# Low parts of half-size weight blocks: a negated copy and an accumulating transfer in place of subtractions on GpSimd

## The chip, the cores and the metric

The kernel runs on one core of one Trainium2 chip. The metric is the device time of one execution in microseconds; the time before is 1047.58 us, the median of three runs (1045.82 to 1047.79).

A core has five engines that run their own instruction queues in order: TensorE (PE, with its weight loads as PEld), VectorE (DVE), ScalarE (ACT), GpSimd (POOL) and SyncE (SP). They wait for each other by semaphores. Transfers run on 16 DMA engines; they are issued by an instruction on the queue of SP or ACT and, after the change, also on that of POOL.

## The reference

One inference step of two layers over 1024 prompt tokens and 8 x 4 sample tokens (1056 columns in all), d_model 1024, in float32. The first layer is a gated linear recurrence (RG-LRU), the second, which the change concerns, an HGRN2 layer:

```python
def _hgrn_layer(x, g_norm, w_in, lb, o_gain, w_out, S0):
    xn = _rmsnorm(x, g_norm)
    u = (xn @ w_in).astype(jnp.float32)          # w_in: 1024 x 4096
    q, f, iv, gate = jnp.split(u, 4, axis=-1)
    q = jax.nn.silu(q).reshape(Bsz, T, H_B, DK_B)            # 8 heads of 128
    ...                                                      # log_g from f and lb; k = -expm1(log_g)
    o, S_T = _hgrn2_chunked(q, k, v, log_g, S0)
    o = o * lax.rsqrt(jnp.mean(o * o, axis=-1, keepdims=True) + EPS) * o_gain...
    y = (o.reshape(Bsz, T, INNER_B) * jax.nn.silu(gate)).astype(x.dtype)
    return x + y @ w_out, S_T.astype(x.dtype)
```

## The kernel before

**Three matmuls for a product.** Float32 products are made from operands of type float32r. Each operand is split into a high part (the value, rounded by a copy to float32r) and a low part (value minus high part). `mm3` (L255 to L257) then adds high x high, high x low and low x high into one PSUM bank. So every block of weights needs a high part `hi` (tile `whi`) and a low part `lo` (tile `wlo`) before PE can use it.

**Weights.** A block comes from HBM into a raw buffer (`wraw`; in the second layer two further raw buffers lie in rows of the tile `R`). ACT copies it to `hi`; POOL (or DVE, at a few places) subtracts `hi` from it into `lo` (`subtract`, L339). `hi` and `lo` have rings of NW = 4 blocks of 512 columns each, used in turn by all blocks. `weights` (with its copy on L394) does this for ordinary products. It is the first layer's way and also that of the output projection at the end.

**Seven products for eight.** From the third head on all four parts of the second layer's input projection, and two of the second head's, are computed by `seven`, 13 calls in all. A call takes two blocks of 128 output rows by 1024 inputs, thus four half-size blocks "11", "12", "21", "22" of 128 x 512. Four combinations of them (`combine`, L1458, on DVE, in the raw buffers themselves; the fifth raw buffer is "s") let seven products stand for eight. The products are numbered 1 to 7; 1 and 2 use "11" and "12" as loaded, 6, 7, 5 and 3 use combined blocks, 4 uses "22". The order is a string such as `126b754b3`, where a `b` is a burst of the attention part of a head. Each product is done twice, over 264 columns (`x` 0 and 1), so a half is 4 x 3 matmuls. `plus` (L1521, DVE) and a copy on ACT (L1493, product 1) empty the PSUM banks, of which three are used in turn for these products.

**The split.** `split(p)` makes the high and low part for product p: a copy on ACT (L1448) and the subtractions on POOL, in CUT = 2 pieces of 256 columns. There are 13 x 7 = 91 splits. The next splits of a call are entered four products ahead, as the ring allows:

```python
for p in steps[2:NW]:
    split(p)
...
n = steps.index(p) + NW
if n < 7:
    split(steps[n])
```

A raw buffer that has had its last split is handed on (`freed`, `rawq`); the next call's loads, issued on ACT's queue, go into it once the split's reads are done. `combine` likewise overwrites a raw buffer only after the splits that read it.

**The order of work.** Nothing is issued in the order in which the code is written. `fl.add(engine, us, emit, reads, writes, priority, kb)` enters each step with an estimated duration (`act`, `dve`, `pool`, `dma`) and what it reads and writes; `Flow.run` plans the start of all steps by these estimates, improves the plan by passes from the end and by a random search, and then emits each engine's instructions in the planned order. One plan covers the first layer, a second one the rest. PE's products keep their order; the other engines' instructions do not.

Of the kernel before, what the change touches and what calls it, by code (L numbers as in the profile page):

```python
# [18 lines left out]
AF = mybir.ActivationFunctionType  # L19
ALU = mybir.AluOpType  # L20
# [3 lines left out]
SEARCH = 3000  # L24
NW, NXO, NRAW = 4, 3, 3
K1 = 5
NMM = 3
HC = 2
NM7 = 3
FQ, GV0, GV = "12b675b43", "126b74b35", "126b754b3"  # L30
CUT = 2
SPOTS, SPOTS0, SPOTS1 = (-1, -1, 0, 2), (2, 5, -1, -1), (1, 5, 9, 13, 17, 20)
K2 = 8 - K1
RM, SM = 3, 6
# [189 lines left out]
def tile_trunk(ctx: ExitStack, tc: tile.TileContext, xT, prm, hc, w0, wg, wo0, w1, wo1, s_in,  # L224
               yT, h_out, c_out, sp_out, ss_out):
    nc = tc.nc
    V, S, G, T, Q = nc.vector, nc.scalar, nc.gpsimd, nc.tensor, nc.sync
# [22 lines left out]
    def chunk(c):  # L250
        return slice(c * CH, (c + 1) * CH)

    def mm3(out, w, xh, xl, first, last):
        wh, wl = w
        T.matmul(out, wh, xh, start=first, stop=False)  # L255
        T.matmul(out, wh, xl, start=False, stop=False)  # L256
        T.matmul(out, wl, xh, start=False, stop=last)  # L257
# [53 lines left out]
    with ExitStack() as l0:  # L311
        pl = l0.enter_context(tc.tile_pool(name="l0", bufs=1, reuse_waits="tile"))
        fl = Flow("PE")

        def fixed(name, shape, dt=F32, pool=None):
            return (pool or pl).tile(shape, dt, tag=name, name=name)
# [7 lines left out]
        def dma(dst, src, r=(), w=(), prio=5, kb=180, q=Q):  # L324
            fl.add("SP" if q is Q else "ACT", 0.45, lambda: q.dma_start(dst, src), r, w, prio, kb * (1.0 if r or fl.exact else 0.75))

        def act(n, emit, r, w, prio=5, more=0.0):
            fl.add("ACT", (0.09 + 0.00088 * n if fl.exact else 0.25 + 0.0007 * n) + more, emit, r, w, prio)

        def dve(n, emit, r, w, prio=5, both=False):  # L330
            own = 0.135 if "scalar_tensor_tensor" in emit.__code__.co_names else 0.085
            fl.add("DVE", own + 0.00107 * n if fl.exact else 0.13 + 0.0011 * n, emit, r, w, prio, both=both)

        def pool(n, emit, r, w, prio=5):
            fl.add("POOL", 0.13 + 0.0022 * n if fl.exact else 0.1 + 0.00245 * n, emit, r, w, prio)

        def subtract(e, n, b, x, a, r, w, prio):

            emit = lambda: e.tensor_tensor(b, x, a.bitcast(F32), op=ALU.subtract)  # L339
            if e is G:  # L340
                pool(n, emit, r, w, prio)
            else:
                dve(n, emit, r, w, prio, True)
# [38 lines left out]
        def weights(src, n, prio=2, e=G, at=None, q=Q, own=()):  # L382

            own = iter(own)
            got = []
            for a in range(0, n, 512):
                m = min(512, n - a)
                raw, *rk = next(own, None) or next(raws)
                if at:
                    (hi, hk), (lo, lk) = ((o[:, a:a + m], k) for o, k in at)  # L390
                else:
                    (hi, hk), (lo, lk) = next(his), next(los)
                dma(raw[:, :m], src[:, a:a + m], (), rk, prio, m / 2, q)
                act(m, lambda hi=hi, raw=raw, m=m: S.copy(hi[:, :m], raw[:, :m]), rk, (hk,), prio)  # L394
                subtract(e, m, lo[:, :m], raw[:, :m], hi[:, :m], (*rk, hk), (lk,), prio)
                got.append((hi, lo, hk, lk))

            def get(k):
                q = slice((k % 4) * 128, (k % 4 + 1) * 128)
                hi, lo, hk, lk = got[k // 4]  # L400
                return hi[:, q], lo[:, q], (hk, lk)

            return get
# [18 lines left out]
        def project0(items):  # L422

            for src, evac in items:
                w = weights(src, 1024)
                for c in range(NCH):
                    evac(c, *product(w, xcols(c)))
                    yield
# [432 lines left out]
        raw = (halves[1][:8], [slots[i] for i in (1, 4, 7, 2, 5, 8)] + [halves[1][8], free[8]], free[:8])  # L861
# [82 lines left out]
    with ExitStack() as l1:  # L944
        p1 = l1.enter_context(tc.tile_pool(name="l1", bufs=1, reuse_waits="tile"))
        last = {e: max(t[3] for t in fl.log if t[1] == e) for e in Flow.ENGINES}
        fl = Flow(side=0.4, busy={e: max(0.0, t - last["PE"]) for e, t in last.items()})
        banks8 = [next(mm) for _ in range(4)] + [next(hg) for _ in range(4)]
        mm, hg = cycle(banks8[:NMM]), cycle(banks8[NMM:])
        ts = cycle(ks)  # L950
# [3 lines left out]
        at = fixed("attn", [128, 8, 128], F32, p1)  # L954
# [30 lines left out]
        def pe(us, emit, r, w):  # L985
            fl.add("PE", us, emit, r, w, 1, main=True)
# [16 lines left out]
        def inherit(new, olds):  # L1003

            fl.readers.setdefault(new, []).extend(i for k in olds for i in (*fl.readers.get(k, ()), *([fl.writer[k]] if k in fl.writer else [])))
# [3 lines left out]
        def ykeys(m, a, n):  # L1009

            return [("Y", m, i) for i, (u, v) in enumerate(zip(CUTS, CUTS[1:])) if u < a + n and v > a]
# [409 lines left out]
        def seven(h, a, b, order, at=()):  # L1421
# [24 lines left out]
            def split(p):  # L1446
                (raw, rk), (hi, hk), (lo, lk) = slot[named[p]], next(his), next(los)
                act(512, lambda: S.copy(hi, raw), (rk,), (hk,), 2)  # L1448
                for i in range(CUT):
                    w = slice(i * (512 // CUT), (i + 1) * (512 // CUT))  # L1450
                    subtract(G, 512 // CUT, lo[:, w], raw[:, w], hi[:, w], (rk, hk), (lk,), 2)
                parts[p] = hi, lo, (hk, lk)
                if p not in (1, 2):
                    freed.append(slot[named[p]])
# [15 lines left out]
            for c in order:  # L1470
# [8 lines left out]
                hi, lo, wk = parts[p]  # L1479
# [36 lines left out]
                n = steps.index(p) + NW  # L1516
# [72 lines left out]
        for k in range(H):  # L1589
            if k < 4:  # L1590
                olds = [("x", 1, k, x) for x in range(2)] + [("T", 1, i, k, x) for i in range(2) for x in range(2)]
            else:
                n, i = ((2, 0), (3, 0), (4, 0), (4, 1))[k - 4]
# [18 lines left out]
        def yparts(c):  # L1612
            return [(yh[k][:, chunk(c)], yl[k][:, chunk(c)], (("yh", k, c), ("yl", k, c))) for k in range(K1)]

# [12 lines left out]

        mm, hg = cycle(banks8[:NMM]), cycle(banks8[NMM:])
        raws = cycle([r for r in rawq if r[1][0] == "raw"])
# [6 lines left out]
        for n, (m, c) in enumerate([(m, c) for c in range(NCH) for m in range(2)] + [(m, c) for m in range(2, KD) for c in range(NCH)]):  # L1636
            if m not in ws2:
                at_ = None
                if m < 2:
                    at_ = [(flat[m + 2, 1][:, i * 640:i * 640 + 640], ("wt", m, i)) for i in range(2)]  # L1640
                    for _, k in at_:
                        inherit(k, [("T", m + 2, 1, j, x) for j in range(4) for x in range(2)])
                ws2[m] = weights(wo1[m][:, :128 * K1], 128 * K1, at=at_)
                for k in ykeys(Y2 + m, 0, TOK):
# [15 lines left out]
        for m in range(KD):  # L1660
            row = (xh, xl)[m // 4][4 + m % 4]
            hi, lo, hk, lk = row[:, :nl], row[:, nl:2 * nl], ("late", m, 0), ("late", m, 1)
            for k in (hk, lk):
                inherit(k, [("x", p, m % 4, x) for p in (2, 3) for x in range(2)])
            raw, rk = next(raws)
            dma(raw[:, :nl], wo1[m][:, 128 * K1:], (), (rk,), 1, nl / 2)
            act(nl, lambda hi=hi, raw=raw: S.copy(hi, raw[:, :nl]), (rk,), (hk,), 1)
# [58 lines left out]
        for a, n in OUT:  # L1726
# [4 lines left out]
            for m in range(KD):  # L1731
# [5 lines left out]
                hi, lo, wk = late[m]  # L1737

                def emit(ps=ps, hi=hi, lo=lo, q=q, n=n):
                    for k in range(K2):  # L1740
                        w = slice(128 * k, 128 * k + 128)
                        mm3(ps[:, :n], (hi[:, w], lo[:, w]), yh[K1 + k][:, q], yl[K1 + k][:, q], k == 0, k == K2 - 1)

                pe(9 * n / 2200, emit, (*wk, *((o, K1 + k, c) for o in ("xh", "xl") for k in range(K2) for c in cs)), (pk,))
                x, xk = x2[m][:, q], ykeys(Y2 + m, a, n)
# [89 lines left out]
```

## The time and the profile before

| | |
|---|---|
| median of 3 runs | 1047.58 us (1045.82 to 1047.79) |
| span of the profiled execution, first to last instruction | 1045.1 us; its own time around the span is not recorded, the three runs lie 0.7 to 2.7 us above the span |
| busy: PE, DVE, ACT, POOL | 1033.6, 824.2, 582.9, 511.3 us |
| first and last start of the changed copy L1448 | 548.2 and 902.0 us |

A row of a group reads: line, engine, operation, output tile <- inputs, shapes, count | busy us, mean ns of one | idle time of the engine just before them, and who ended it. A row of waits reads: who waited, for whom: us in total, times, longest. A row of the timeline begins with its start and its length in us. Transfers have the size in KB and the median time from issue to landing in us. The table of stretches gives each engine's busy time with its number of instructions.

### The profile page before, as it was taken

The page shows a single profiled execution, that of the slowest core. Times are in us where ns is not written, and L with a number is a line of the kernel's source. Part 1 is how long each engine was busy: PE and PEld are TensorE (multiplying, and loading weights), DVE is VectorE, ACT ScalarE, POOL GpSimd, SP SyncE. Part 2 cuts the span into 40 slices and gives each one's busy share as a digit, 9 for nine tenths or more (in the row PEclk, how much of TensorE's full clock was granted, in tenths as well). Part 3 has the DMA queues.
Part 4 walks back from the last instruction along what each step waited for, and adds up shares of the span by engine and source line. Part 5 has one row for each costly group of instructions (what it writes and reads, how often), then busy time and mean ns, then how long its engine had stood idle before and what let it go on. Part 6 is the DMA issues. An engine that isn't in the chain of part 4 may idle for free.

```text
span 1045.1 us, 25638 instructions
## 1 busy us (share of the span) xinstructions
PE 1033.6 (99%) x9860; PEld 1004.5 (96%) x9860; DVE 824.2 (79%) x1620; ACT 582.9 (56%) x1327; POOL 511.3 (49%) x587
## 2 busy tenths in 40 slices
PE   9999999999999999999999999999999999999997
PEld 9999999999999999999999999999999999999986
DVE  7999996788788689345598998988979797985436
ACT  6568656867765776334455464546463645652324
POOL 3425343544435365644517655555555565651544
PEclk9999999999999999999999999999999999999998
DMA  9201112123761586435646142423324242576204
GB/s 303 66 20 55 54 49 72 49 65 97 214 197 48 170 281 195 145 118 173 195 138 187 56 131 97 129 85 116 97 101 127 88 127 85 182 224 210 86 1 167
DMA packets 92010, 130.67 MB, mean 125 GB/s; under 512 B 11632, under 2 KB 70000, under 8 KB 91888
## 3 DMA queue, kind: packets, MB, share of 16 engines
q1 hardware_dynamic: 82096, 112.64, 34.7%
q10 hardware_dynamic: 9792, 16.40, 5.0%
q8 instruction: 77, 1.26, 0.5%
q14 instruction: 45, 0.37, 0.1%
HBM read 85.93 MB, written 38.20 MB: 119 GB/s over the span
## 4 chain that ended last, share of the span: by engine, by line
PE 88%; DVE 8%; DMA 2%; issue 1%; POOL 0%; ACTq 0%; ACT 0%; POOLq 0%; SPq 0%; DVEq 0%
PE mm L255 25%; PE mm L257 24%; PE mm L256 24%; PE hg L1075 2%; PE hg L583 1%; PE hg L1289 1%; DMA wraw<-in_w_dram 1%; PE hg L255 1%; PE hg L1291 1%; PE hg L256 1%; PE hg L257 1%; DVE a L1257 1%; DVE sg L1057 1%; DVE R L1057 1%; PE hg L1333 1%
## 5 line engine op out<-in xcount | busy, mean ns | idle before, releaser
L255 PE MATMUL mm<-xh,whi 128*128 128x352 f32 (+1 forms) x1127 | 352.5, 313 | 0.7 <-DVE k L1521 0.5
L257 PE MATMUL mm<-xh,wlo 128*128 128x352 f32 (+1 forms) x1127 | 346.9, 308 | 0.0
L256 PE MATMUL mm<-xl,whi 128*128 128x352 f32 (+1 forms) x1127 | 346.7, 308 | 0.0
L339 POOL TENSOR_TENSOR wlo<-wraw,whi 128x256 fp32r<-128x256 f32 (+3 forms) x188 | 203.9, 1100 | 207.1 <-ACT whi L394 103.0
L255 PEld LDWEIGHTS mm<-xh,whi 128*128 128x128 f32 x1127 | 211.7, 188 | 3.2 <-DVE k L1521 1.6
L256 PEld LDWEIGHTS mm<-xl,whi 128*128 128x128 f32 x1127 | 212.0, 188 | 1.5
L257 PEld LDWEIGHTS mm<-xh,wlo 128*128 128x128 f32 x1127 | 211.8, 188 | 0.0
L255 PE MATMUL mm<-t,whi 128*128 128x264 f32 (+1 forms) x330 | 96.5, 292 | 0.8 <-DVE k L1521 0.8
L515 DVE SCALAR_TENSOR_TENSOR k<-xb,prm_sb,k 128x352 f32<-128x352 f32 (+2 forms) x144 | 89.5, 633 | 9.6 <-ACT k L512 6.4
L257 PE MATMUL mm<-t,wlo 128*128 128x264 f32 (+1 forms) x330 | 94.5, 286 | 0.0
L256 PE MATMUL mm<-t,whi 128*128 128x264 f32 (+1 forms) x330 | 94.3, 286 | 0.0
L339 POOL TENSOR_TENSOR wlo<-R,whi 128x256 fp32r<-128x256 f32 x70 | 63.7, 931 | 47.6 <-ACT whi L1448 30.7
L1521 DVE TENSOR_TENSOR k<-mm,k 128x264 f32<-128x264 f32 x154 | 64.2, 423 | 16.5 <-PE mm L257 15.8
L598 POOL TENSOR_TENSOR k<-X 128x352 f32<-128x352 f32 x36 | 42.8, 1199 | 47.7 <-DVE R L599 38.8
L255 PEld LDWEIGHTS mm<-t,whi 128*128 128x128 f32 x330 | 62.0, 188 | 1.6 <-DVE k L1521 1.0
L257 PEld LDWEIGHTS mm<-t,wlo 128*128 128x128 f32 x330 | 62.1, 188 | 0.2 <-POOL wlo L339 0.2
L256 PEld LDWEIGHTS mm<-t,whi 128*128 128x128 f32 x330 | 62.1, 188 | 0.0
L394 ACT CAST whi<-wraw 128x512 fp32r<-128x512 f32 (+2 forms) x79 | 43.8, 572 | 29.9 <-PE mm L256 15.9
L1448 ACT CAST whi<-wraw 128x512 fp32r<-128x512 f32 x56 | 34.4, 616 | 33.2 <-DVE wraw L1458 13.5
L255 PE MATMUL mm<-yh,whi 128*128 128x352 f32 x153 | 49.9, 326 | 0.0
L257 PE MATMUL mm<-yh,wlo 128*128 128x352 f32 x153 | 49.4, 323 | 0.0
L256 PE MATMUL mm<-yl,whi 128*128 128x352 f32 x153 | 49.4, 323 | 0.0
(457 smaller groups left out, 2540.3 us busy)
## 6 DMA issues: line engine op xcount, KB each, us to landing
wraw<-in_w_dram SPq DMA_DIRECT2D x53, 256.0 KB, 3.1
wraw<-in_w_dram ACTq DMA_DIRECT2D x37, 256.0 KB, 2.9
wraw<-in_wo_dram SPq DMA_DIRECT2D x34, 192.0 KB, 2.5
R<-in_w_dram ACTq DMA_DIRECT2D x17, 256.0 KB, 2.9
si<-in_s_in_dram SPq DMA_DIRECT2D x8, 512.0 KB, 6.6
vt<-sg SPq DMA_DIRECT2D x8, 512.0 KB, 3.1
sg<-vt SPq DMA_DIRECT2D x32, 128.0 KB, 3.0
kt<-kt SPq DMA_DIRECT2D x8, 512.0 KB, 2.6
```

The source lines that it names most:

```text
L255: T.matmul(out, wh, xh, start=first, stop=False)
L256: T.matmul(out, wh, xl, start=False, stop=False)
L257: T.matmul(out, wl, xh, start=False, stop=last)
L339: emit = lambda: e.tensor_tensor(b, x, a.bitcast(F32), op=ALU.subtract)
L394: act(m, lambda hi=hi, raw=raw, m=m: S.copy(hi[:, :m], raw[:, :m]), rk, (hk,), prio)
L515: dve(u, lambda src=src, dst=dst, sh=sh, k=k: V.scalar_tensor_tensor(dst, sh(src, k), pc("cw", 12 * k + m), dst, op0=ALU.mult, op1=ALU.add ...
L583: fl.add("PE", 0.62, lambda ps=ps, i=i, c=c: T.matmul(ps[:96, :CH], gs[:, i, :], ST[:96, chunk(c)], start=True, stop=True), (("gs",), *((" ...
L598: pool(CH, lambda x=x, a=a, b=b: G.tensor_tensor(x, a.bitcast(F32), b.bitcast(F32), op=ALU.add), (ak, bk), (xk,), 3)
L1057: dve(n // 2, lambda sv=sv, dv=dv, s=s, f=f: V.tensor_tensor(dv[:, :, s, :], sv[:, :, s, :], f, op=ALU.mult), (*sk, *gk), dk if i == o els ...
L1075: T.matmul(ps[32 * j:32 * j + 32, n * w:n * w + w], B[:, o:o + 32], q(slice(o, o + 32)), start=True, stop=True, tile_position=(0, 32 * j))
L1448: act(512, lambda: S.copy(hi, raw), (rk,), (hk,), 2)
L1521: dve(QT, lambda: V.tensor_tensor(o[0], z[0], u[0], op=ALU.add), (z[1], u[1]), (o[1],), 0)
```

## The change

`split` no longer subtracts on POOL. ACT writes the negated raw block into `lo` (a second pass over the 512 columns, which does not need `hi` as an input), rounded as the high part is; then a transfer issued on POOL's queue adds the raw block to it, within SBUF. `remainder` and `swdge` are new; the plan counts 1.1 us of POOL for the issue, and for the landing what it counts for other transfers. The raw buffer is now read by the transfer, so it is free when that has landed. A branch in `weights` that would do the same stays off, as `FIRST` is true.

```diff
+FIRST = True
...
+        def swdge(dst, src, r, w, prio, kb, op=None):
+            more = {"accum_op": op} if op else {}
+            fl.add("POOL", 1.1, lambda: G.dma_start(dst, src, **more), r, w, prio, kb)
+
+        def remainder(n, lo, raw, r, lk, prio):
+
+            act(n, lambda: S.activation(lo, raw, AF.Copy, scale=-1.0), r, (lk,), prio)
+            swdge(lo, raw, (*r, lk), (lk,), prio, n / 2, ALU.add)
...
-                subtract(e, m, lo[:, :m], raw[:, :m], hi[:, :m], (*rk, hk), (lk,), prio)
+                if e is G and at is None and not FIRST:
+                    remainder(m, lo[:, :m], raw[:, :m], rk, lk, prio)
+                else:
+                    subtract(e, m, lo[:, :m], raw[:, :m], hi[:, :m], (*rk, hk), (lk,), prio)
...
             def split(p):
                 (raw, rk), (hi, hk), (lo, lk) = slot[named[p]], next(his), next(los)
                 act(512, lambda: S.copy(hi, raw), (rk,), (hk,), 2)
-                for i in range(CUT):
-                    w = slice(i * (512 // CUT), (i + 1) * (512 // CUT))
-                    subtract(G, 512 // CUT, lo[:, w], raw[:, w], hi[:, w], (rk, hk), (lk,), 2)
+                remainder(512, lo, raw, (rk,), lk, 2)
                 parts[p] = hi, lo, (hk, lk)
```

## The prediction

> **What bounds the kernel now.** I read the page first, then the table of stretches, then who waited for whom on PE in the stretch that the change touches.
>
> ```profile
> span 1045.1 us, 25638 instructions
> PE 1033.6 (99%) x9860; PEld 1004.5 (96%) x9860; DVE 824.2 (79%) x1620; ACT 582.9 (56%) x1327; POOL 511.3 (49%) x587
> core 0: us, PE busy (x) PEld busy (x) DVE busy (x) ACT busy (x) POOL busy (x), PEclk, DMA share, GB/s
> 548.00:908.00 360.00, 359.30 (x5036) 346.40 (x5035) 312.16 (x644) 190.68 (x505) 206.62 (x245) 1.00 0.36 115
> 908.00:950.00 42.00, 40.09 (x570) 38.02 (x569) 35.52 (x79) 19.62 (x60) 18.73 (x21) 1.00 0.64 196
> ```
>
> TensorE has work in 99% of the span. All 91 splits that are changed start between 548 and 902 us. In the stretch 548 to 908 PE is idle for 0.70 of 360 us, at a granted clock of 1.00. DVE is next (312 us), then POOL (207) and ACT (191). So POOL, which the change relieves, doesn't set the end; relief can reach the time only through PE's waits. First the stretch's own, then those of 905 to 923 us:
>
> ```profile
> PE mm L255 <- DVE k L1521: 0.5, 2, 0.2
> PEld mm L255 <- DVE k L1521: 1.6, 4, 0.5
> PE mm L255 <- DVE k L1521: 1.9, 2, 1.1
> PEld mm L255 <- ACT whi L394: 1.3, 1, 1.3
> PEld mm L255 <- DVE k L1521: 1.0, 1, 1.0
> ```
>
> In the stretch PE waited four times for a PSUM bank that DVE had not emptied (L1521), at most 1.6 us in all as the weight loads show it. Behind it come two waits, 1.3 + 1.0 = 2.3 us. The most that any relief can give is 1.6 + 2.3 = 3.9 us.
>
> **The change part by part.** First what is removed and what stands for it, by kind and shape:
>
> ```profile
> L339 POOL TENSOR_TENSOR wlo<-wraw,whi 128x256 fp32r<-128x256 f32 x112 | 102.1, 931 | 95.7 <-ACT whi L1448 73.0 <-PE mm L257 7.0 <-DVE a L1257 4.8
> L339 POOL TENSOR_TENSOR wlo<-R,whi 128x256 fp32r<-128x256 f32 x70 | 63.7, 931 | 47.6 <-ACT whi L1448 30.7 <-PE mm L257 6.3 <-PE hg L1333 4.0
> L1317 POOL TENSOR_TENSOR rst<-rst,mhalf 128x4 f32<-128x4 f32 x12 | 12.2, 1015 | 11.5 <-DVE rst L1315 11.5
> L1448 ACT CAST whi<-wraw 128x512 fp32r<-128x512 f32 x56 | 34.4, 616 | 33.2 <-DVE wraw L1458 13.5 <-PE mm L256 12.7 <-PE mm L257 4.4
> L1448 ACT CAST whi<-R 128x512 fp32r<-128x512 f32 x35 | 21.7, 621 | 28.5 <-PE mm L256 17.2 <-POOL wlo L339 6.0 <-PE mm L257 4.4
> ```
>
> - Removed: 112 + 70 = 182 subtractions on POOL, 102.1 + 63.7 = 165.8 us, two for each of the 91 splits.
> - Added on ACT: 91 passes of the shape of the high part's copy. 34.4 + 21.7 = 56.1 us is what 91 of those take, so ACT goes from 191 to about 247 us of 360 (69%). It lies beside PE's work; ACT also empties some banks (L1493) and issues the weight loads, so its queue is a rival below.
> - Added on POOL: 91 transfer issues. No row shows GpSimd issuing a transfer. The bounds are 0.33 us (an issue on ACT's queue, quoted below) and 1.86 (the two subtractions that it replaces). I take 1.0, by L1317: 1015 ns for 4 elements per partition, so nearly all fixed cost. POOL then falls from 207 to about 207 - 166 + 91 = 132 us.
> - Added to the DMA engines: 91 x 256 KB = 23.9 MB, 66 GB/s over 360 us beside the 115 in the table. By bytes the DMA share goes from 0.36 to 0.57, or to 0.78 if reading the destination counts as much again. This leaves room, but single loads will land later than now.
>
> The landing time of an accumulating transfer is shown by no row either. The nearest:
>
> ```profile
> wraw<-in_w_dram ACTq DMA_DIRECT2D x37, 256.0 KB, 2.9
> si<-in_s_in_dram SPq DMA_DIRECT2D x8, 512.0 KB, 6.6
> vt<-sg SPq DMA_DIRECT2D x8, 512.0 KB, 3.1
> R<-td SPq DMA_DIRECT2D x72, 44.0 KB, 1.9
> ```
>
> Bounds are 1.9 us (44 KB within SBUF) and 6.6 (the slowest of 512 KB here). I take 3.1: 256 KB of source and 256 KB of destination are to be read, and 512 KB out of SBUF land in 3.1. So a low part is ready 2 x 0.617 + 1.0 + 3.1 = 5.3 us after ACT starts, and 5.6 with two hand-offs of about 0.15 (in the rows below ACT ends at 680.88 + 0.61 and POOL starts at 681.63). The bounds give 1.23 + 0.33 + 1.9 = 3.5 and 1.23 + 1.86 + 6.6 = 9.7.
>
> The Trainium skill (DMA: Bandwidth & Descriptors, Anatomy of one DMA — SWDGE (gpsimd) path) fits such a transfer by about 2.0 us plus its bytes over 436 GB/s. By that, an estimate from this page, 256 KB take 2.6 us and the low part is ready after some 4 us; the sum would be 0.3 us less. No run here shows it.
>
> What has this delay to fit into? I paired the 91 splits in order with the 91 products (each two halves of twelve 264-column matmuls). First the first and the last pair, then the three kinds that are tightest: a split at the start of the stage, a third product of a seven, and a sixth.
>
> ```profile
> 548.24 0.62 ACT L1448 CAST whi<-R 128x512 fp32r<-128x512 f32 x1
> 560.85 0.28 PE L255 MATMUL mm<-xh,whi 128*128 128x264 f32 x1
> 902.00 0.62 ACT L1448 CAST whi<-R 128x512 fp32r<-128x512 f32 x1 [1.27 <-PE mm L256]
> 917.68 0.29 PE L255 MATMUL mm<-xh,whi 128*128 128x264 f32 x1
> 561.41 1.13 ACT L1448 CAST whi<-wraw 128x512 fp32r<-128x512 f32 x2
> L255 PE MATMUL mm<-t,whi x2: 283/284/285, 566.7 to 567.1; 128*128 128x264 f32 x2
> 669.09 0.61 ACT L1448 CAST whi<-wraw 128x512 fp32r<-128x512 f32 x1
> L255 PE MATMUL mm<-t,whi x3: 283/285/287, 677.0 to 677.8; 128*128 128x264 f32 x3
> 680.88 0.61 ACT L1448 CAST whi<-wraw 128x512 fp32r<-128x512 f32 x1
> 681.63 1.24 POOL L339 TENSOR_TENSOR wlo<-wraw,whi 128x256 fp32r<-128x256 f32 x1 [3.27 <-PE mm L1095]
> L255 PE MATMUL mm<-t,whi x2: 283/284/285, 687.5 to 687.9; 128*128 128x264 f32 x2
> ```
>
> From ACT's start to the first matmul there are 12.6 us at the first pair and 15.7 at the last. The tight ones have 566.7 - 561.4 = 5.3 (once), 687.5 - 680.9 = 6.6 (four like it) and 677.0 - 669.1 = 7.9 (six or seven). A delay of 5.6 us fits everywhere but the first of these, where 0.3 us is lost. The cover for the whole added latency is the ring of four high and low blocks: three other products are computed meanwhile. Without it each split would cost PE 5.6 us.
>
> The gain: DVE's two-input operations take longer beside POOL's reads. The same operation on 512 columns, in two places:
>
> ```profile
> 671.90 0.68 DVE L1458 TENSOR_TENSOR R<-R,wraw 128x512 f32<-128x512 f32 x1
> 799.25 2.62 DVE L1458 TENSOR_TENSOR wraw<-wraw,R 128x512 f32<-128x512 f32 x1
> ```
>
> With 166 us of POOL's reads gone, the four waits for L1521 should go: -1.6. I leave the 2.3 us behind the stage as they are, because POOL's subtractions there belong to other weights (L394) and stay.
>
> The sum against this execution: 1045.1 - 1.6 + 0.3 = 1043.8 us of span. The runs lie 0.7 to 2.7 us above that span (1045.82 to 1047.79); their median of 1047.58 lies 2.5 above, which I carry over: **1046.3 us**, 0.12% less than before. That is inside the 0.2%, about 2.1 us, that a measurement of this kernel can tell from no change.
>
> A rule speaks against transfers issued by GpSimd. DVE rows of plain copies in this stretch are few:
>
> ```profile
> L1143 DVE COPY attn<-hg 64x256 f32<-64x256 f32 x7 | 3.0, 426 | 0.1
> ```
>
> The Trainium skill (SBUF — State Buffer, SBUF: two separate sides) says that GpSimd can't write descriptors while DVE runs a copy in a two-port mode. If this row's copies, which read PSUM, count at all, an issue waits 0.43 us at most: 0.4 us more at the one tight split, 1046.7 in all. No run here shows such a wait.
>
> **The rivals.**
>
> *Relief reaches further (faster).* All 3.9 us of DVE- and ACT-made waits go: 1047.58 - 3.9 = 1043.7 us. For it: DVE is the second busiest engine, and all that slows it in the last microseconds of the stretch is carried on. Against: both waits behind the stage stand beside POOL work that stays, and the weights loaded there get their raw buffers later.
>
> *Queues block in order (slower).* A raw buffer is released only when the transfer has read it. ACT's queue issues the next weight load into it and stands still until then; the bank copies L1493 and the next splits are behind it.
>
> ```profile
> 684.06 0.33 ACTq L325 DMA_DIRECT2D wraw<-in_w_dram  x1
> 684.44 0.62 ACT L1448 CAST whi<-R 128x512 fp32r<-128x512 f32 x1 [2.94 <-POOL wlo L339]
> ACT k L1493 <- POOL wlo L339: 4.5, 4, 1.1
> ```
>
> Now a release comes 684.06 - 680.88 = 3.2 us after the split starts; with 5.6 it comes 2.4 later. Before L1493 ACT stood still four times, 1.1 us; that becomes 1.1 + 2.4 = 3.5, and the copy itself takes about 0.4. PE has three banks, so it can run two halves on: four triples of matmuls at (677.8 - 677.0) / 2 = 0.4 us make 1.6 us a half, 3.2 in all. So 0.7 us a time; if a release that the order of work takes for earlier hits one copy in half of the 13 calls, 6.5 x 0.7 = 4.6 us, and 1046.3 + 4.6 = 1050.9 us. It decides once releases come over 3.2 - 1.1 - 0.4 = 1.7 us later than now. Against it: the order is planned anew with the transfer's latency in it, so other work can stand ahead of a late load. DVE's combinations (L1458) that overwrite a raw buffer wait for the same release, so the same holds for DVE's queue and its L1521.
>
> *The transfer lands at its upper bound (slower).* With 9.7 us the first tight split costs 4.4, the four at 6.6 cost 3.1 each and seven at 7.9 cost 1.8 each: 4.4 + 12.4 + 12.6 = 29 us if nothing moves. An earlier start can give back about half: 1046.3 + 15 = 1061 us. It decides from 6.6 us on.
>
> *The change reaches less than its words.* With FIRST true the branch in `weights` isn't taken; only the 91 splits change. That is what the sum above counts, so no time of its own hangs on it.
>
> **How the numbers follow.** The forecast has 0.48: the delay fits by rows, but two of its terms are bounded only. Relief that reaches further has 0.14, blocked queues 0.26, a late landing 0.12. Faster by over 0.2% is the first rival, 0.14; slower are the two others, 0.38; the rest is 0.48. The forecast's own range is 1045.5 to 1049.6. The whole range starts at 1044.6, inside the faster case, and ends at 1058: it takes in the blocked queues and the nearer part of a late landing, and leaves out about 2 in 10.
>
> **What would show it.** Right: POOL's busy time between 548 and 908 falls to 110 to 150 us, ACT's rises to about 247, the L1458 rows come near 0.68 us, PE's idle time there stays under 1.5 us, and a transfer lands within about 4 us of its issue. Wrong: rows of PE or PEld waiting for a DMA into wlo (late landing), or PE waits for ACT k L1493 or DVE k L1521 with ACT idle before a load (blocked queues). Anything that moves before 548 us would contradict the reading that only the second layer changes.

## The result and the profile after

The changed kernel is slower: 1056.07 us (median of 4 runs, 1054.58 to 1059.82) against 1046.87 us (1045.82 to 1047.79) for the kernel before, here the median of four runs, one more than ahead of the prediction; a ratio of 1.0091 [1.0076, 1.0106], or 9.2 us by the medians. The profiled execution took 1057.54 us. Its stage ahead of the splits, 0 to 548 us, is as good as unchanged (PE busy for 545.65 us there, 546.20 before). In the code after, the lines have moved: the high part's copy is L1461 (was L1448), ACT's negated copy L334, the transfer's issue L330, loads L326, `combine` L1469 (was L1458), `plus` L1532 (was L1521), product 1's bank copy on ACT L1504 (was L1493), the matmuls of `mm3` L256 to L258.

The page of the kernel after, its span and busy times; then its table of stretches (columns as in the prediction):

```profile
span 1055.8 us, 25608 instructions
PE 1035.2 (98%) x9860; PEld 1004.5 (95%) x9860; DVE 782.0 (74%) x1620; ACT 629.0 (60%) x1418; POOL 435.0 (41%) x496
```

```profile
548.00:908.00 360.00, 350.52 (x4891) 336.38 (x4890) 263.60 (x622) 229.10 (x578) 124.37 (x148) 1.00 0.70 167
548.00:918.00 370.00, 360.52 (x5028) 346.15 (x5027) 270.79 (x640) 236.66 (x596) 129.03 (x154) 1.00 0.71 170
918.00:1055.80 137.80, 129.06 (x1153) 121.43 (x1151) 78.86 (x180) 52.13 (x148) 58.61 (x66) 0.97 0.46 147
```

POOL has 76 us less work, ACT 46 us more, the clock is the same, and yet PE idles for 9.48 of 360 us where it idled for 0.70. The second row shows how far that goes: PE now needs 370 us for about as many matmuls (5028) as it did in 360 before (5036). What follows it, 137.8 us, is about as long as before (137.1). So the loss lies in the stretch of the changed splits. Who made PE wait there, 540 to 925 us (who waited, for whom: us in total, times, longest):

```profile
PE mm L256 <- DVE k L1532: 5.2, 5, 2.0
PE mm L258 <- DMA wlo<-R: 1.7, 1, 1.7
PE mm L258 <- DMA wlo<-wraw: 1.4, 3, 0.5
PE hg L1088 <- issue: 0.9, 1, 0.9
```

More than half (5.2) are PSUM banks that DVE emptied too late; 3.1 us are low parts that had not landed. Next the added work, from the groups of the page (busy, mean ns | idle before), then the transfers (median us from issue to landing) and the transfers' queue (packets, MB, share of 16 engines' time):

```profile
L330 POOL DMA_DIRECT2D wlo<-wraw x56 | 48.8, 877 | 138.3 <-ACT wlo L334 110.7
L330 POOL DMA_DIRECT2D wlo<-R x35 | 30.8, 879 | 86.0 <-ACT wlo L334 69.2
L334 ACT ACTIVATE wlo<-wraw 128x512 fp32r<-128x512 f32 x56 | 35.0, 627 | 29.4 <-DVE wraw L1469 9.5
q0 software_dynamic: 13104, 23.86, 13.3%
wlo<-wraw POOLq DMA_DIRECT2D x56, 256.0 KB, 3.9
wraw<-in_w_dram ACTq DMA_DIRECT2D x37, 256.0 KB, 3.7
wlo<-R POOLq DMA_DIRECT2D x35, 256.0 KB, 4.4
```

An issue and a pass cost about what was expected. The landing does not: 3.9 and 4.4 us, where the plan counts at least 2.4 + 256/600 = 2.83 from its start. And these are medians. One transfer follows, from its issue to the wait of PE; first what the line L330 says of that transfer (issued at 620.07), then the semaphore wait on ACT's queue ahead of a load (ns, min/median/max; start), then the timeline (start, length, engine, line; in brackets the idle time before and who ended it):

```profile
DMA to landing us min/median/max: 8.4/8.4/8.4
L326 ACTq EVENT_SEMAPHORE  x1: 7413/7413/7413, 621.1 to 621.1; - x1
620.07 0.85 POOL L330 DMA_DIRECT2D wlo<-wraw  x1 [3.12 <-ACT R L1546]
622.18 0.61 ACT L1461 CAST whi<-R 128x512 fp32r<-128x512 f32 x1
628.53 0.33 ACTq L326 DMA_DIRECT2D wraw<-in_w_dram  x1
628.97 0.63 ACT L334 ACTIVATE wlo<-R 128x512 fp32r<-128x512 f32 x1 [6.17 <-issue]
632.41 0.25 ACT L1218 COPY vts<-mm 32x128 f32<-32x128 f32 x1
632.69 0.29 DVE L1216 TENSOR_TENSOR vst<-mm,vst 32x128 fp32r<-32x128 f32 x1 [4.49 <-ACT vts L1218]
633.75 0.43 DVE L1532 TENSOR_TENSOR k<-mm,k 128x264 f32<-128x264 f32 x1
634.24 0.39 PE L256 MATMUL mm<-xh,whi 128*128 128x264 f32 x1 [1.30 <-DVE k L1532]
```

The transfer holds the raw buffer until it lands at 620.07 + 8.4 = 628.5. ACT's queue has a load into a freed raw buffer, and stands at its semaphore for 7.4 us. It issues the load at 628.53, when that transfer has landed (ACT stood idle for 6.17 us until then; the timeline puts this down to "issue", as it names no releaser). Only then does ACT run the next passes, the `kt` copies (L1205) and the copies out of PSUM that end with `vts` (L1218). DVE stood 4.49 us for `vts`; behind that operation in DVE's queue is `plus`, which empties a bank at 633.75; and PE, 1.30 us late, writes that bank at 634.24. In this chain ACT and DVE stand idle, for 6.17 and 4.49 us, with work of their own in the queue. Four of PE's five waits for `plus` (1.3, 0.8, 0.7 and 0.5 us) come right behind such a wait of DVE for `vts`; the kernel before has no wait of DVE at that operation (L1203 there).

The fifth and longest has another last step, a combination that DVE can't start before a transfer has landed:

```profile
701.39 0.90 DVE L1469 TENSOR_TENSOR wraw<-wraw 128x512 f32<-128x512 f32 x1 [2.65 <-DMA wlo<-wraw]
706.98 0.43 DVE L1532 TENSOR_TENSOR k<-mm,k 128x264 f32<-128x264 f32 x1
707.46 0.39 PE L256 MATMUL mm<-xh,whi 128*128 128x264 f32 x1 [2.01 <-DVE k L1532]
```

After it DVE works off what has queued up, and reaches `plus` at 706.98. So both next users of a held raw buffer, ACT's load and DVE's combination, stand behind waits of PE.

### The profile page after: what moved, and what is told of

It is laid out like the page before. It is cut to its first block, busy times and chain, and to the rows that moved or that the text cites. A ratio compares the mean times of both kernels' runs of the same rounds, so it can differ in the third digit from the quotient of the medians.

```text
span 1055.8 us, 25608 instructions
## 1 busy us (share of the span) xinstructions
PE 1035.2 (98%) x9860; PEld 1004.5 (95%) x9860; DVE 782.0 (74%) x1620; ACT 629.0 (60%) x1418; POOL 435.0 (41%) x496
## 3 DMA queue, kind: packets, MB, share of 16 engines
q0 software_dynamic: 13104, 23.86, 13.3%
## 5 line engine op out<-in xcount | busy, mean ns | idle before, releaser
L256 PE MATMUL mm<-xh,whi 128*128 128x352 f32 (+1 forms) x1127 | 352.6, 313 | 5.2 <-DVE k L1532 5.2
L258 PE MATMUL mm<-xh,wlo 128*128 128x352 f32 (+1 forms) x1127 | 346.8, 308 | 0.0
L256 PEld LDWEIGHTS mm<-xh,whi 128*128 128x128 f32 x1127 | 211.7, 188 | 8.0 <-DVE k L1532 6.3
L258 PEld LDWEIGHTS mm<-xh,wlo 128*128 128x128 f32 x1127 | 211.8, 188 | 0.0
L349 POOL TENSOR_TENSOR wlo<-wraw,whi 128x512 fp32r<-128x512 f32 (+1 forms) x76 | 102.9, 1365 | 105.6 <-ACT whi L404 94.6
L330 POOL DMA_DIRECT2D wlo<-wraw x56 | 48.8, 877 | 138.3 <-ACT wlo L334 110.7
L258 PE MATMUL mm<-t,wlo 128*128 128x264 f32 (+1 forms) x330 | 94.9, 288 | 3.2 <-DMA wlo<-R 1.7
L528 DVE SCALAR_TENSOR_TENSOR k<-xb,prm_sb,k 128x352 f32<-128x352 f32 (+2 forms) x144 | 89.8, 635 | 11.1 <-ACT k L525 7.9
L256 PE MATMUL mm<-t,whi 128*128 128x264 f32 (+1 forms) x330 | 96.5, 292 | 0.1
L1532 DVE TENSOR_TENSOR k<-mm,k 128x264 f32<-128x264 f32 x154 | 64.0, 424 | 22.1 <-PE mm L258 20.2
L330 POOL DMA_DIRECT2D wlo<-R x35 | 30.8, 879 | 86.0 <-ACT wlo L334 69.2
L258 PEld LDWEIGHTS mm<-t,wlo 128*128 128x128 f32 x330 | 62.1, 188 | 4.3 <-DMA wlo<-R 2.3
L256 PEld LDWEIGHTS mm<-t,whi 128*128 128x128 f32 x330 | 62.0, 188 | 0.9 <-ACT k L1504 0.3
L334 ACT ACTIVATE wlo<-wraw 128x512 fp32r<-128x512 f32 x56 | 35.0, 627 | 29.4 <-DVE wraw L1469 9.5
L256 PE MATMUL mm<-yh,whi 128*128 128x352 f32 x153 | 49.9, 326 | 0.0
L258 PE MATMUL mm<-yh,wlo 128*128 128x352 f32 x153 | 49.4, 323 | 0.0
```

Source lines behind the costliest of these rows:

```text
L330: fl.add("POOL", 1.1, lambda: G.dma_start(dst, src, **more), r, w, prio, kb)
L334: act(n, lambda: S.activation(lo, raw, AF.Copy, scale=-1.0), r, (lk,), prio)
L528: dve(u, lambda src=src, dst=dst, sh=sh, k=k: V.scalar_tensor_tensor(dst, sh(src, k), pc("cw", 12 * k + m), dst, op0=ALU.mult, op1=ALU.add ...
L1532: dve(QT, lambda: V.tensor_tensor(o[0], z[0], u[0], op=ALU.add), (z[1], u[1]), (o[1],), 0)
```

## The experiments

The theory: the transfer lands later than planned and holds its raw buffer, and work that is queued in order behind a step that needs the buffer stands still. Two steps need it: DVE's combinations (the theory's first wording had these) and ACT's weight loads. The rivals: low parts land too late for PE itself; the DMA engines' added traffic slows the other transfers; or the new plan is just a worse draw of its random search. (Where the expectations use letters, A is the held buffer with DVE's combinations, A2 the same with ACT's loads, B the late low parts, C the traffic and D the 91 further passes.) Ratios are to the kernel before on the same chip, with 95% intervals.

| run | us | ratio |
|---|---|---|
| e1_no_transfer | 1045.30 | 0.9979 [0.9968, 0.9989] |
| e2_sub123 | 1053.33 | 1.0052 [1.0036, 1.0068] |
| e3_sub4567 | 1046.53 | 0.9992 [0.9982, 1.0001] |
| e4_plan_late | 1051.60 | 1.0038 [1.0023, 1.0053] |
| e5_traffic | 1080.70 | 1.0326 [1.0284, 1.0367] |
| e6_plain | 1046.45 | 0.9991 [0.9981, 1.0000] |
| e7_loads_sp | 1045.38 | 0.9983 [0.9974, 0.9992] |
| e8_after_seed | 1062.19 | 1.0140 [1.0105, 1.0175] |
| e9_before_loads_sp | 1046.22 | 0.9988 [0.9980, 0.9997] |
| e10_loads_sp_seed | 1051.07 | 1.0035 [1.0022, 1.0049] |
| e11_loads_sp_late | 1062.78 | 1.0147 [1.0133, 1.0161] |
| e12_before_seed | 1052.22 | 1.0047 [1.0034, 1.0059] |
| e13_same_order_sp | 1046.57 | 0.9992 [0.9983, 1.0001] |
| e14_not_held | 1051.72 | 1.0039 [1.0026, 1.0053] |

**The passes alone.** The transfer is left out, so the low part lacks the sum.

```diff
-            swdge(lo, raw, (*r, lk), (lk,), prio, n / 2, ALU.add)
```

> The change with the accumulating transfer left out: ACT still writes the negated block into the low part, GpSimd does nothing for the splits, and the low part lacks the sum. Theory A (the transfers hold raw buffers and DVE stands still before it may overwrite them), theory B (low parts come too late for PE) and theory C (the transfers' traffic makes the other loads late) all expect the whole loss gone, and with GpSimd's reads gone too at most the forecast's relief: 1043 to 1047 us. Theory D (the 91 further ACT passes) expects most of the loss to stay: 1052 to 1056.

Faster than before by 0.21%, about 2.2 us. In the table of stretches of this run PE idles for 0.67 us:

```profile
548.00:908.00 360.00, 359.33 (x5039) 346.82 (x5038) 276.81 (x648) 239.15 (x600) 43.21 (x64) 1.00 0.37 113
```

ACT's 91 passes (ACT 239 us) cost nothing that can be seen. The whole loss belongs to the transfer and what it brings with it. The gain of some 2 us is of the size of the relief forecast, but without the transfer the order is planned anew too, so the run doesn't show that it is the relief.

**Which products' transfers.** One run keeps POOL's subtractions for products 1, 2 and 3, the other for 4 to 7. The raw buffers of 1, 2 and 3 are the ones that a combination overwrites (after 3 it is one of the next call, as that buffer becomes its "s"; only after the first call's 3 it is a load); those of 4 to 7 go on to the next call's loads (after the first call, that of 5 becomes the "s").

```diff
-                remainder(512, lo, raw, (rk,), lk, 2)
+                if p in (1, 2, 3):               # the other run: (4, 5, 6, 7)
+                    for i in range(CUT):
+                        ...                      # subtract on POOL, as before
+                else:
+                    remainder(512, lo, raw, (rk,), lk, 2)
```

> Splits of products 1, 2 and 3 subtract on GpSimd as before; 4, 5, 6 and 7 use pass and transfer. DVE's combinations overwrite only raw buffers whose last readers are splits 1, 2 and 3, so theory A expects no row of DVE waiting for a transfer into wlo and 1048 to 1051 us. Theory B expects PE's waits for wlo (3.1 us in the changed kernel) to stay at 4/7 or more, and 1052 to 1054. Theory C has 4/7 of the traffic: 1046.9 + 4/7 x 9.2 = 1052 us, with DVE's share of waits falling no faster than that.

> The other half: splits 1, 2 and 3 use pass and transfer, 4 to 7 subtract on GpSimd. Theory A keeps its whole price, 5 of 9 us: 1052 to 1055, with DVE waiting for transfers about as often as in the changed kernel (9 times, 16.6 us). Theory B expects 1048 to 1050 (products 1 and 2 have the longest lead). Theory C has 3/7 of the traffic: 1046.9 + 3/7 x 9.2 = 1050.8.

With transfers on 4 to 7 more than half of the loss stays (1.0052); with transfers on 1 to 3 none does (0.9992). The times by themselves don't decide: 1053.33 us is what the rivals with late low parts and with traffic expected of the first run, and 1046.53 is below what any of the three expected of the second. In the second run, DVE's combinations did wait for landings, and it cost nothing (waits of the run with 4 to 7 subtracted):

```profile
DVE R L1474 <- DMA wlo<-R: 4.7, 2, 3.1
DVE wraw L1474 <- DMA wlo<-wraw: 2.1, 2, 1.4
```

In the first run, no combination waited for a landing, but ACT did, 8.1 us in all (waits of the run with 1 to 3 subtracted; the three largest of five):

```profile
ACT xh L1405 <- DMA wlo<-wraw: 2.1, 1, 2.1
ACT kt L1321 <- DMA wlo<-R: 2.0, 2, 1.2
ACT vst L1214 <- DMA wlo<-wraw: 2.0, 1, 2.0
```

None of these ACT lines reads `wlo`: the wait is that of a load ahead of them in ACT's queue. In the second run ACT stood so only once (4.6 us, at 578 us, in the time of the first call), at no cost. So combinations that wait don't make the loss by themselves; ACT's loads are the likelier way. Both runs have orders of their own, so this is a pointer and not yet a proof.

**A plan that knows the landing.** The plan counts the landing 1.5 us later and twice the time for its bytes.

```diff
+LATE = 1.5
-                dma = max(dma + kb / 250.0, t0 + 2.4 + kb / 600.0)
+                sw = e == "POOL"
+                dma = max(dma + kb / (125.0 if sw else 250.0), t0 + 2.4 + kb / 600.0 + (LATE if sw else 0.0))
```

> The changed kernel, with only the plan's count for the accumulating transfer changed: landing 1.5 us later and twice the time on the DMA engines for its bytes. Instructions are the same, their order differs. If the loss is that the order takes the transfer for earlier than it is (A or B by way of the plan), other work stands ahead of the waits: 1047 to 1051 us and DVE's waits for transfers under 5 us. If it is the traffic or the latency itself (C), no order mends it: 1054 to 1058.

1.0038: a good half of the loss goes, and what stays is of another kind. PE idles for 1.64 us between 548 and 908. Its largest wait lies behind, at 923 us, for an activation of the output projection that DVE splits:

```profile
PE mm L258 <- DVE t L351: 2.5, 1, 2.5
```

So the wrong estimate seems to be a part of the cause: with a later landing planned, other work can stand ahead of the loads, and the waits of ACT that the profile puts down to a transfer into `wlo` fall from 16.0 to 6.3 us (540 to 925 us). But the order of everything after is changed with it (the granted clock of the last 142 us is 0.96 and 0.95, where it was 1.00 and 0.97), so this run alone doesn't tell how much.

**Traffic by itself.** The kernel before, with a plain transfer of 256 KB from HBM to HBM issued by GpSimd for each split.

```diff
+                fl.add("POOL", 1.1, lambda: G.dma_start(spill[0], wa[:, :512]), (hk,), (), 2, 256)
```

> The kernel before, with a plain transfer of 256 KB for each split added, issued by GpSimd: the call's first half-size block from HBM to a scratch tensor in HBM. Nothing waits for it and it holds no buffer; it adds the transfers' traffic and GpSimd's issues alone, and the plan knows of it. If traffic alone makes the loss (C): 1051 to 1056 us, with the weight loads at 3.6 us or more. If the loss comes from what waits for the accumulating transfer (ACT's and DVE's queues, PE for the low part): 1046 to 1049, even where loads land later.

1.0326, but that can't be put down to traffic: all transfers write the same scratch block, and GpSimd stood still until its own earlier one had landed. The first of the run's POOL waits in the whole span:

```profile
POOL spill L1454 <- DMA spill<-in_w_dram: 96.7, 42, 7.9
```

The run says nothing about traffic. It is a case of the same kind on another engine: a queue waits for 97 us for transfers ahead of its other work, in a kernel that takes 33 us longer.

**A plain transfer in the same order.** Only the addition is left out: the transfer overwrites the low part with the raw block. The order on all engines is that of the changed kernel.

```diff
-            swdge(lo, raw, (*r, lk), (lk,), prio, n / 2, ALU.add)
+            swdge(lo, raw, (*r, lk), (lk,), prio, n / 2)
```

> The changed kernel with a plain transfer in place of the accumulating one: the raw block lands in the low part (rounded on the way), the sum is left out. Same instructions, same order, same waits. If the accumulating itself is what makes the transfer slow on the DMA engines (1.9 times the time per byte of the other queues in the changed kernel), it lands in 3.0 to 3.4 us and the time is 1047 to 1051. If the latency is that of any transfer from GpSimd beside this traffic, landing stays at 3.9 to 4.4 and the time at 1054 to 1058.

0.9991: the loss is gone, with the same bytes and the same instructions. The transfers of this run, and their queue:

```profile
q0 software_dynamic: 13104, 23.86, 7.7%
wlo<-wraw POOLq DMA_DIRECT2D x56, 256.0 KB, 2.9
wlo<-R POOLq DMA_DIRECT2D x35, 256.0 KB, 3.6
```

A landing takes 1.0 and 0.8 us less. The packets' time is 7.7% of 16 x 1045.0 us, 98 ns for each of 13104, against 13.3% of 16 x 1055.8 us, 171 ns, when they accumulate. The place shown above, in this run's timeline:

```profile
626.23 0.33 ACTq L326 DMA_DIRECT2D wraw<-in_w_dram  x1
626.66 0.63 ACT L334 ACTIVATE wlo<-R 128x512 fp32r<-128x512 f32 x1 [4.26 <-PE mm L258]
630.39 0.29 DVE L1216 TENSOR_TENSOR vst<-mm,vst 32x128 fp32r<-32x128 f32 x1 [2.34 <-ACT vts L1218]
631.45 0.43 DVE L1532 TENSOR_TENSOR k<-mm,k 128x264 f32<-128x264 f32 x1
```

ACT's queue stands still here too, for 5.5 us, as this transfer took 6.5 us. But the load goes out 7.6 us after the pass on ACT has started and not 9.5 (the whole place comes 0.4 us earlier here), DVE waits 2.34 instead of 4.49 us, `plus` comes at 631.45, and PE doesn't wait. The standstill is not lost time in itself: PE doesn't wait behind the shorter one at this place, and does behind the one that is 1.9 us longer.

**The loads on another queue.** The `seven` calls' weight loads are issued by SP instead of ACT, and planned so.

```diff
-                dma(t, src, (), (k,), 2, 256, S)
+                dma(t, src, (), (k,), 2, 256)
```

> The changed kernel with the weight loads of the seven-product calls issued on SP's queue and not on ACT's, so that a load that waits for a raw buffer no longer stops ACT. Theory A2 (ACT's queue stands still before a load whose raw buffer a transfer still reads): 1048 to 1052, no row of ACT waiting for a transfer into wlo. Theory B (low parts late) and C (traffic): 1054 to 1058. A price of its own is possible: SP's queue then stands still before other transfers.

The loss is gone (0.9983) though the transfers land no sooner (4.3 and 4.6 us) and the DMA engines are as busy (a share of 0.74 between 548 and 908, 13.7% of the span for the transfers' queue). In this order, then, neither the traffic nor the landing time as such costs anything. The expectation, 1048 to 1052 us, was too high.

The same edit on the kernel before, as a control:

> Control for the run with the loads on SP's queue: the kernel before, GpSimd subtracting, with the same loads moved to SP. If the move is what mends the changed kernel (ACT no longer stopped by a raw buffer that a transfer still reads), it does little here, where a buffer is released by GpSimd within 2 to 3 us: 1045 to 1048 us. If moving the loads is a gain of its own that merely covers the transfers' price, this comes out near 1047.5 - 10 = 1038 or at least under 1043.

0.9988 [0.9980, 0.9997]. There the move is worth 1.2 us by the medians; on the changed kernel it is worth 11.

**Another draw of the plan's search.** `Random(1)` becomes `Random(2)` in the changed kernel, in the one with loads on SP, and in the kernel before.

```diff
-        rng = Random(1)
+        rng = Random(2)
```

> The changed kernel with another seed in the plan's random search: the same instructions in another order, with the same estimates. It tells how much of the 9 us hangs on one order. If the loss is what the transfers cost under any order planned by these estimates, 1053 to 1059; if it is the luck of one order, it can lie anywhere from 1045 to 1060, and a single run near 1047 would show that.

> The changed kernel with the loads on SP's queue, with another seed of the plan's search. If the queue is the cause, the order matters little: 1044.5 to 1048 us, against 1062 for the changed kernel under the same seed. If the first such run was one lucky order, 1052 to 1062.

> The kernel before with the other seed: how far the order of work alone moves a kernel without the transfers. If orders differ by as much as the changed kernel's two (6 us), 1042 to 1055; if the waits for transfers make an order fragile, 1046 to 1049 here.

1062.19, 1051.07 and 1052.22 us. The first two lie outside what was expected, because the second draw costs the kernel before, too, 5 us by itself (its first changed copy starts at 552.8 us and not at 548.2, so that loss lies ahead of the splits). Within one draw the differences agree: changed minus before +9.2 and +10.0 us; changed minus loads on SP 10.7 and 11.1 us. The second draw of the changed kernel spreads widely (1057.49 to 1064.82 us), so this agrees to a few us and no closer; but both draws show the loss and what the move gives back, and it is not one bad draw.

**Loads on SP and a later planned landing.** The two edits together, with 1.0 us.

> The changed kernel with the loads on SP's queue and the plan counting the accumulating transfer as landing 1.0 us later, with twice the time for its bytes. If what is left after the move is waits that the order takes for shorter than they are, 1043 to 1045 us; if nothing is left to mend, 1044.5 to 1047, as without it.

1.0147, far above the 1043 to 1047 us expected. PE's waits in its stretch:

```profile
PE mm L260 <- DMA wlo<-R: 7.0, 3, 2.5
PE mm L260 <- DMA wlo<-wraw: 4.4, 2, 2.2
```

Here the rival is seen at work: low parts land too late for PE itself, five times, in different calls. In those looked at, a combination stands late and three transfers of a call are issued at one go (three between 702.3 and 705.0 us, for example). It is a real danger of the change, which in the changed kernel itself makes 3.1 us of waits.

**The same order, another issuer.** This is the sharpest test. The plan is that of the changed kernel, down to each step, and PE, DVE and POOL run the same order; the loads keep their planned place on ACT, but SP issues them.

```diff
-        def dma(dst, src, r=(), w=(), prio=5, kb=180, q=Q):
-            fl.add("SP" if q is Q else "ACT", 0.45, lambda: q.dma_start(dst, src), ...)
+        def dma(dst, src, r=(), w=(), prio=5, kb=180, q=Q, on=None):
+            fl.add("SP" if q is Q else "ACT", 0.45, lambda: (on or q).dma_start(dst, src), ...)
...
-                dma(t, src, (), (k,), 2, 256, S)
+                dma(t, src, (), (k,), 2, 256, S, Q)
```

> The changed kernel with its own plan and order; the loads of the seven-product calls are planned as on ACT, at the same places, but issued on SP's queue. If ACT's standstill before a load whose raw buffer is still being read makes the loss: 1046 to 1050 us, and no row of ACT waiting for a transfer into wlo. If DVE's standstill before its combinations makes it: 1053 to 1057, with DVE's 16.6 us of such waits unchanged.

0.9992 [0.9983, 1.0001]: the loss is gone. The table of stretches of this run, its transfers, and DVE's waits from 540 to 908:

```profile
548.00:908.00 360.00, 358.77 (x5024) 345.57 (x5024) 274.76 (x639) 237.46 (x594) 128.01 (x154) 1.00 0.73 174
wlo<-wraw POOLq DMA_DIRECT2D x56, 256.0 KB, 4.3
wlo<-R POOLq DMA_DIRECT2D x35, 256.0 KB, 4.7
DVE wraw L1469 <- DMA wlo<-wraw: 11.9, 9, 2.2
DVE R L1469 <- DMA wlo<-R: 4.2, 2, 2.1
DVE vst L1216 <- ACT vts L1218: 1.7, 6, 0.3
```

The landings are even longer than in the changed kernel (by 0.4 and 0.3 us), the combinations wait as long for them (16.1 us; 9.5 + 7.1 = 16.6 there), the DMA share is as high (0.73). What has gone is ACT's standstill: no wait of ACT is put down to a transfer into `wlo` any more (16.0 us in the changed kernel), and DVE's waits for `vts` are 1.7 us, those for `kt` (L1321) 11.6 instead of 17.6. In the changed kernel, and in the run with the plain transfer, the same row reads (one line of each):

```profile
DVE vst L1216 <- ACT vts L1218: 16.6, 6, 4.5
```

```profile
DVE vst L1216 <- ACT vts L1218: 7.1, 6, 3.6
```

16.6, 7.1 and 1.7 us in the same order of work on DVE: the first loses some 9 us, the other two nothing that can be measured. Most of the 3.1 us of late low parts go by the same edit, as this run has 0.5 us of them with slower landings: a pass on ACT that is held up has its transfer issued late. And PE no longer waits for `plus` at all, though the combination that held it up at 707 us still waits 0.96 us for its landing. So ACT's standstill makes the loss. What no run separates is how much of it passes through DVE's wait for `vts` and how much through blocks that ACT loads and splits late.

**The buffer not held.** The changed kernel, but each transfer adds one fixed block of the weights from HBM instead of the raw buffer, so no load waits for a transfer. The part that is changed: the low parts of products 2 to 7 add another block than their own.

```diff
-            swdge(lo, raw, (*r, lk), (lk,), prio, n / 2, ALU.add)
+            swdge(lo, raw if src is None else src, (*r, lk), (lk,), prio, n / 2, ALU.add)
...
-                remainder(512, lo, raw, (rk,), lk, 2)
+                remainder(512, lo, raw, (rk,), lk, 2, wa[:, :512])
```

> The changed kernel in its own order, but each transfer adds the call's first half-size block from HBM and not the raw buffer (for products 2 to 7 the low part is then of another block): it lands about as late (3.5 to 4.5 us) but holds no raw buffer. If held buffers make the loss, by ACT's or DVE's queue: 1045 to 1048 us, no waits of ACT or DVE for a transfer into wlo. If low parts that come too late for PE make it: 1052 to 1057, with PE's waits for wlo at 3 us or more.

1.0039: 43% of the loss stays. No wait of ACT or DVE for a transfer into `wlo` is left, and DVE waits 1.7 us for `vts`. But the source is now HBM, and all transfers of the stretch take longer; PE waits for low parts (transfers, then PE's largest wait from 540 to 925):

```profile
wlo<-in_w_dram POOLq DMA_DIRECT2D x91, 256.0 KB, 4.9
wraw<-in_w_dram ACTq DMA_DIRECT2D x37, 256.0 KB, 5.0
PE mm L258 <- DMA wlo<-in_w_dram: 2.3, 3, 1.8
```

With the buffer not held, about 5 us come back in spite of slower transfers. The profiled execution, 1049.41 us, is the fastest of the five, so its waits are less than those of the median. How much of the rest is the source in HBM stays open, since a second buffer in SBUF for the block was not tried.

## Why the prediction was wrong

The forecast was 1046.3 us, no change. It is slower by 9.2 us: the direction was missed. The time lies above the forecast's own range (to 1049.6) and within the whole one (to 1058), between the blocked queues' 1050.9 and the late landing's 1061. The rival that names the mechanism had 0.26.

- **The bound was right, and the relief in kind.** PE's idle time is what counts. The DVE combinations (L1458) took 0.98 us in the mean before and 0.70 after, near the 0.68 that the forecast named as a sign. The run without the transfer gains 2.2 us where the forecast took off 1.6, within the 3.9 at the most; that this is the relief is likely, but its order differs too.
- **POOL and ACT were right.** POOL fell by 511.3 - 435.0 = 76.3 us; the sum was 166 - 91 = 75. An issue took 0.88 us (1.0 taken). A pass took 0.627 us; ACT rose by 46.1 us, where 56.1 was counted, and its busy time alone cost nothing (the runs without the transfer and with the loads on SP). The DMA share of 0.70 lies between the two ends given.
- **The landing was the first term that was mis-sized.** 3.1 us was taken from the 512 KB row; the medians are 3.9 and 4.4, and the transfer shown took 8.4, above the upper bound of 6.6. The estimate from the Trainium skill (DMA: Bandwidth & Descriptors, Anatomy of one DMA — SWDGE (gpsimd) path), 2.6 us, is near what the plain transfer took (2.9 and 3.6), and 1.3 to 1.8 us below the accumulating one: the page's figure has no term for the addition. The forecast's sum compared a single typical delay with the leads, and has no term for a landing of 8.4 us.
- **The cover was right, for the products alone.** With 0.7 to 1.2 us more delay, PE's direct waits for low parts are 3.1 us; with ACT's queue free they are 0.5. In this order the ring of four blocks covers an even slower transfer, as the forecast said; the run with the loads on SP and a later planned landing has another order where it doesn't (11.4 us).
- **The step that failed is the one that put the held raw buffer among the rivals.** The forecast's sum follows the low part and not the buffer. Where it priced the buffer it counted only the bank copies of product 1 (now L1504) behind a standing load: 0.7 us a time, 4.6 in all. What stood behind it in the trace were also the next splits, which the forecast names but gives no price, the `kt` copies, and the PSUM copies for which DVE waits; DVE's `plus` is behind those. So its price was half of what the same order gives back when SP issues the loads: 1056.07 against 1046.57 us (ratios of 1.0091 and 0.9992 to the kernel before, about 10 us). It wasn't added to the sum either. The point from which it decides, a release 1.7 us later than before (3.2 us after the split begins), was exceeded already by the forecast's own 5.6, which is 2.4 later; and in the case shown, ACT starts the pass at 619.05 and the load goes out at 628.53, 9.5 us after, 6.3 more than those 3.2.
- **What spoke against that rival did not hold.** "The order is planned anew with the transfer's latency in it": the plan has 2.83 us for it where its own count of the DMA engines' work doesn't make it more (the formula in the diff of the plan that knows the landing). The forecast's own 3.1, and most of its range of 1.9 to 6.6, lay above that. Counting 1.5 us more and twice the time for the bytes took over half of the loss away, though in another order.
- **The late landing as a rival** was right that PE would wait for a DMA into `wlo`, but this is the smaller share (3.1 of 9.48 us), and most of it goes with ACT's standstill. The rule on GpSimd being locked out while DVE copies (the Trainium skill, SBUF — State Buffer, SBUF: two separate sides) shows no sign here: all issues in the stretch took 0.85 to 1.21 us, so if such a wait lengthens an issue, none is above 0.36. With so few plain copies the runs neither confirm nor refute it.
- Of the signs named, PE's waits for `plus` with ACT idle before a load came as written for blocked queues; PE's idle time, 9.48 us against less than 1.5, refuted the forecast. POOL's 124 us between 548 and 908 lie within the 110 to 150 named.

The runs also point to a version that is faster than the kernel before, if barely: the change with the loads on SP's queue, 1045.38 us, 0.9983 [0.9974, 0.9992]. Its interval overlaps with that of the kernel before with the same move (0.9988 [0.9980, 0.9997]), so the gain can't be put down to the change.

## What to carry to other kernels

When a copy by an engine becomes a transfer, follow the source buffer as well as the result: whoever fills that buffer next now waits for the landing, and if the fill is issued on a queue that also computes, everything behind it waits too. Price a standstill by all that is queued behind the waiting instruction, on its engine and on the next, rather than by the one copy that comes to mind; and check the latency that a plan assumes against the slowest landings, not the median. Issue loads that may wait from a queue that computes nothing.

## What was not expected of the hardware

- An accumulating transfer within SBUF takes 1.7 times the packet time of a plain one (171 against 98 ns for each of 13104 packets, 23.86 MB) and lands 0.8 to 1.0 us later in the same order of work. Its issue on GpSimd takes 0.88 us instead of 0.54.
- Landings of transfers of one size spread widely: in the stretch 3.3 us at the least, 4.2 in the middle and 8.9 at the most; the plain ones 2.3, 3.1 and 8.7.
- A DMA share of 0.73 (the same order, loads issued by SP) and 0.74 (loads on SP, planned so) in a stretch cost nothing by itself; the kernel before had 0.36.
